# A two-block network on one core: grouped transposes, paired split products and a new order of the last expert visits, with an earlier router load and a merged final norm

## The chip, the cores and the metric

The kernel runs on one core of a Trainium2 chip. The time is that of one execution on the device, in microseconds (us), and the figure to compare is the median of several runs. The core has five engines with instruction queues of their own: TensorE (PE in the rows, with its weight loads as PEld), VectorE (DVE), ScalarE (ACT), GpSimd (POOL) and SyncE (SP), which issues almost all DMAs here. TensorE's clock has two levels, 2.4 and 1.2 GHz; the rows give the granted share (1.00 and 0.50).

## The reference, cut to what matters

A sequence of 256 tokens of width 1024 goes through two blocks of two layers each; every layer is a mixer and a feed-forward, each with a norm before it and a gated residual after it. Layer 0 has a Hyena and neighbourhood-attention mixer with a SwiGLU; layer 1 has a Fourier mixer and a mixture of experts; layers 2 and 3 have a retention and an S5 mixer, each followed by a feed-forward with a short convolution. The parts that the change touches are the mixture of experts

```python
top_val, top_idx = lax.top_k(logits, 2)              # logits: h @ w_router + b_router, 8 experts
for e in range(8):                                   # w1, w3: 1024 x 3584, w2: 3584 x 1024
    out = out + gate[..., e:e+1] * ((silu(h @ w1[e]) * (h @ w3[e])) @ w2[e])
```

and the end, `rms_norm(x) * final_norm_g`. All inputs are float32.

## The kernel before, in words

The residual stream stays in SBUF as `xT`, eight tiles of 128 channels by 256 tokens. Nearly all weights come from memory once, in tiles of about 1 MB through rings of buffers. Products at full width are split: a float32 operand becomes a rounded high part (ScalarE, `Copy` into float32r) and a remainder (VectorE, `tensor_sub`), and three float32r products replace one float32 product.

**The planner.** `Sched` records the operations of a segment, with a cost and the buffers that each reads and writes, and `flush` writes them out in the order of a list schedule: each engine takes the recorded operation that can start first, and of those that can start now the one recorded first. `matmuls` records several TensorE calls as one operation, which nothing can be put between; a `transpose` that is recorded alone is an operation of its own, with a cost of 0.065 us and 0.1 us until the next one that writes the same PSUM bank. Engines then run the emitted order in their queues, one instruction after the other.

**The experts.** With the token counts of these inputs `moe_usual` runs. It is one list of 56 visits, `VISITS`, a visit being one expert and one seventh of its hidden width: four 1 MB tiles of w1 and w3 (`up`), and two of w2, worked in `down` after the next visit's `up`. Tiles pass through 12 buffers in the order of the visits (`listed`, `used`); SyncE issues the load of tile n+12 when tile n's buffer comes free. Tokens are gathered by expert into blocks. A block of 64 tokens (T = 2) or 32 (T = 4) is the stationary operand of float32 products that use 64 or 32 columns of the array, so that two or four run side by side; `hid` records them in groups of two contraction tiles, and so does `down`. Experts 0, 3, 4, 5 have a 64-token block, experts 0, 1, 2, 6, 7 a 32-token block. Experts 1 and 2 have 128 more tokens each, whose products are split: `quarters` cuts a weight tile in four, each with a high and a low half in two of the eight `mwh` buffers, and records three products (`thirds`) for each, into the banks `h0`, `h1` in `up` and `h2`, `h3` in `down`. Between the two, the hidden values `gg` of a block are transposed in bank `t`, two or four transposes a block, and copied to `gt` (`ys` for the big blocks). After an expert's seventh visit `scatter` adds its result to `xT`, with the help of `spread`.

**Before and after the experts.** `fourier` is the segment that comes ahead of them; `route` computes the logits in it. There the router's weights `wr` go into a tile with the tag `posi`, which the tiles `odd` and the positions `posi` use before it; GpSimd clears it, then SyncE loads it. TensorE first uses it in eight products that add the shift's share of the logits to `br`; the products with `w_four` stand behind these in TensorE's order. At the other end of the kernel `finish` is a segment of its own after the last feed-forward: eight squares on ScalarE, eight products with a matrix of ones, a square root, a reciprocal, eight scalings on VectorE, and two DMAs of four tiles each.

Of the kernel before, what the change touches and what calls it, by code (L numbers as in the profile page):

```python
# [24 lines left out]
NE = 8  # L25
# [3 lines left out]
LANE = (0, 0, 0, 1, 0, 1, 1, 1)  # L29
CAPS = (3, 5, 5, 2, 2, 2, 1, 1)  # L30
VISITS = [int(c) for c in "0017031733170317317031734170"
          "4264426042644265265526552655"]


def top(e):
# [266 lines left out]
class Sched:  # L302
# [68 lines left out]
    def matmuls(self, calls):  # L371

        mm = self.tc.nc.tensor.matmul

        def run():
            for o, a, b, st, sp in calls:
                mm(_real(o), _real(a), _real(b), start=st, stop=sp, skip_group_check=True)  # L377

        if self.direct:
            run()  # L380
            return
        op = Op()
        op.eng, op.func, op.fn = "PE", None, run
        op.cost, op.lat = sum(self.cost(self.T, "matmul", c[:3], {})[0] for c in calls), 0.1
        self.add(op, [c[1] for c in calls] + [c[2] for c in calls], [c[0] for c in calls])

    def add(self, op, ins, outs):
# [172 lines left out]
class Net:  # L560
# [613 lines left out]
    def fourier(self):  # L1174
        I = self.I
        with self.segment("fourier", dict(mm=7, rt=1), pools=(1,)) as (p,):
            V, A = self.V, self.A
            cs = self.load(p, "cs", [128, 2, L])
            cl = self.load(p, "cl", [128, 2, 512])
            self.ada_until(1, 2)  # L1180
            a, b = self.scale_cols(self.mods[1], 1, self.normg[:, 2], "modA"), self.mods[1][:, 0:8]
            x, xa = self.xT, p.tile([128, 8, L], F32, name="h")
            A.activation(self.small.tile([128, 1], F32, name="warm"), x[:, 6, 0:1], AF.Sqrt, scale=0.0, bias=self.eps)
            X = p.tile([128, 4, 2, L], F32, name="fA")
            y = self.hilo(p, 8, "fy", "fy")
            sums = self.ps("rt")
            first = []
            for k in range(8):
                sq = self.small.tile([128, L], F32, name="sq", bufs=2)
                V.tensor_scalar(xa[:, k], x[:, k], a[:, k:k + 1], None, op0=OP.mult)  # L1190
                A.activation(sq, x[:, k], AF.Square)
                self.S.matmuls([(sums[:, t:t + 1], sq[:, t * 128:t * 128 + 128], self.ones[:, 0:1],
                                 k == 0 and t == 0, k == 7) for t in range(2)])
                if k % 2:
                    ps = self.ps()
                    for t in range(2):
                        self.mg(ps[:, t * L:t * L + L], [(xa[:, c, t * 128:t * 128 + 128], cs[:, c % 2])
                                                         for c in (k - 1, k)])
# [12 lines left out]
            for g in range(4):  # L1211
                ps = self.ps()
                B = [b[:, 2 * g + k:2 * g + k + 1] for k in range(2)]
                self.mg(ps[:, 0:L], [(X[:, g, tck, 0:128], cl[:, tck, 0:L]) for tck in range(2)], last=False)
                self.mg(ps[:, 0:1], [(cs[:, k, 0:128], B[k]) for k in range(2)], first=False)
                self.mg(ps[:, L:], [(X[:, g, tck, 128:256], cl[:, tck, L:]) for tck in range(2)])
                m_ = mid[32 * g:32 * g + 1]
                self.mg(m_[:, :L], [(X[:, g, tck, 128:129], cl[:, tck, 0:L]) for tck in range(2)], last=False)
                self.mg(m_[:, 0:1], [(cs[:, k, 128:129], B[k]) for k in range(2)], first=False)
                odd = p.tile([128, L], F32, name="odd", tag=("posi", "ang")[g % 2])  # L1220
                A.activation(odd, ps[:, L:], AF.Copy)
                V.memset(odd[0:1], 0.0)
                for k, op in enumerate((OP.add, OP.subtract)):
                    t = self.small.tile([128, L], F32, name="fsum")
                    V.tensor_tensor(t, ps[:, :L], odd, op)
                    if k:
                        A.activation(t[0:1], mid[32 * g:32 * g + 1, :L], AF.Copy)
                    self.put(y, 2 * g + k, t)
            self.rotary(p)
            self.s5_params(p)  # L1230
            self.ada_until(1, 3)
            route = self.route(p) if self.upto > 3 else iter(())
            next(route, None)
            self.ready = ready
            self.dense(I["w_four"], y, 8, lambda m, ps: self.residual(m, ps, 1, 2), fill=self.filler("four"))
            if self.upto > 3:
                self.moe_ahead(*self.rings)
            next(route, None)
# [99 lines left out]
    def moe_usual(self, xg, y, oh, xs, whs):  # L1338

        nc, V, A, mo, T_ = self.nc, self.V, self.A, self.mo, self.T
        S, bank, mix, ident = self.S, self.bank, self.mix, self.ident
        for e in range(1, NE):
            self.which[e] = nc.values_load(mo["ints"].real()[0:1, 1, e:e + 1], engines=(ET.SP,), min_val=0, max_val=NE - 1)
# [76 lines left out]
                                                                                       t % (T // 2) * nw + nw],  # L1422
                            i == 0, i == 7) for i in (kk, kk + 1) for t in range(T)])

        def quarters(w):

            for i in range(4):
                v = w.fold(2048)[:, 512 * i:512 * i + 512]
                h, lo = whs[turn_of("wh", 8)], whs[turn_of("wh", 8)]
                A.activation(h, v, AF.Copy)  # L1430
                V.tensor_sub(lo, v, h.bitcast(F32))
                yield i, h, lo

        def thirds(hi, lo, wh, wl):
            return [(hi, wh), (lo, wh), (hi, wl)]
# [1 line left out]
        def up(e, s):  # L1437
# [6 lines left out]
            for half in range(2):  # L1444
                for k, b, ps in st:
                    hid(k, b, ps, half, w[2 * half:2 * half + 2])
                if e in (1, 2):
                    for j in range(2):
                        for i, h, v in quarters(w[2 * half + j]):
                            kk = 4 * half + i  # L1450
                            self.mg(bank[("h0", "h1")[j]], thirds(big[0][:, kk], big[1][:, kk], h, v),
                                    first=kk == 0, last=kk == 7)
                self.used()
            for k, b, ps in st:
                gg, r, nw = self.gg[1][b // 2], rows(b), 1024 // k.T
# [8 lines left out]
        def down(e, s, st):  # L1464
            w = [self.place(self.at + i) for i in range(2)]
            for k, b, _ in st:
# [1 line left out]
                c = turn_of("gt", 2)  # L1468
                gt, ps = self.gt[:, c], bank["t"]
                m = 4 if T == 2 else 2  # L1470
                for j in range(m):
                    T_.transpose(ps[:, j * 64:j * 64 + 64], gg[r, j * 128:j * 128 + 128], ident[r, r])
                V.tensor_copy(gt[:, :64 * m], ps[:, :64 * m])
                ps = bank["a2"]
                for kk in range(0, 4, 2):
# [8 lines left out]
                    V.tensor_add(k.y, k.y, ps[:, :nd])  # L1484
            if e in (1, 2):
                ps, gg, g = bank["t"], self.gg[0][s % 2], mix["ys"][:, 0]
                for j in range(4):
                    T_.transpose(ps[:, j * 128:j * 128 + 128], gg[:, j * 128:j * 128 + 128], ident)
                A.activation(g[:, 0], ps, AF.Copy)
                V.tensor_sub(g[:, 1], ps, g[:, 0].bitcast(F32))  # L1490
                for j in range(2):
                    for i, h, v in quarters(w[j]):
                        c, d = divmod(i + 4 * j, 2)
                        q = slice(128 * c, 128 * c + 128)
                        self.mg(bank[("h2", "h3")[d]], thirds(g[:, 0, q], g[:, 1, q], h, v),
                                first=s == 0 and c == 0, last=s == 6 and c == 3)
            self.used()
            if s == 6:
                scatter(e)
# [1 line left out]
        def spread(e, k, q):  # L1501
# [8 lines left out]
            else:  # L1510
                dup = o[:, :, 0:128]
            ps = bank["t"]
            for t in range(2):
                T_.transpose(ps[:, t * 128:t * 128 + 128], dup[:, t], ident)
            self.mg(ps[:, L:L + 1], [(dup[:, t], mo["gate"][:, t, e:e + 1]) for t in range(2)])
            V.tensor_copy(mix["gs"][:, q:q + 1], ps[:, L:L + 1])
            V.tensor_copy(ots[q], ps[:, :L])
# [164 lines left out]
    def route(self, pr):  # L1682
# [2 lines left out]
        ranks = self.load(pr, "ranks", [128, NE])  # L1685
        caps = self.load(pr, "caps", [128, NE])
        prior = self.load(pr, "prior", [128, NE])
        wr = pr.tile([128, 8, 32], F32, name="w_rout", tag="posi")
        self.G.memset(wr, 0.0)
        self.Q.dma_start(wr[:, :, 0:NE], I["w_rout"])  # L1690
        br = pr.tile([128, NE], F32, name="br")
        self.Q.dma_start(br, I["b_rout"].to_broadcast([128, NE]))
        self.ada_until(1, 5)
# [270 lines left out]
    def conv_ffn(self, l, fill=None):  # L1964
        layer = 2 + l
        V, A = self.V, self.A
        with self.segment("conv", dict(mm=8), wh=1, pools=(1, 3)) as (p, pb):
# [21 lines left out]
            if l == 0:  # L1989
                fill(32)  # L1990
                self.enter(3, 0, None, [self.I["s5_in"][t] for t in range(AHEAD)])

    def rotary(self, p):
        I, V, A = self.I, self.V, self.A
# [233 lines left out]
                self.s5()  # L2228

    def finish(self):  # L2230
        with self.segment("fin", dict(mm=2)) as _:
            if self.upto >= 10:
                r = self.rstd(self.xT)
                for k in range(8):
                    self.V.scalar_tensor_tensor(self.xT[:, k], self.xT[:, k], self.normg[:, 5, k:k + 1], r,
                                                op0=OP.mult, op1=OP.mult)
            for k in range(0, 8, 4):
                self.Q.dma_start(self.out[:, k:k + 4], self.xT[:, k:k + 4])

    def run(self):  # L2240
        with self.stack:
# [16 lines left out]
            if self.upto > 5:  # L2258
                with self.phase("b"):
# [2 lines left out]
                        self.block2()  # L2262
                    if self.upto > 8:
                        self.conv_ffn(1)
            self.finish()
# [15 lines left out]
```

## Time and profile before

| | |
|---|---|
| median of 3 runs | 2314.18 us (2305.22 to 2314.53) |
| the profiled execution | 2310.9 us, span of the profile 2309.1 us, granted clock 0.97 |
| TensorE busy | 2181.6 us (94%) |
| VectorE, ScalarE, GpSimd busy | 1489.3, 983.7, 22.1 us |
| memory read | 644.7 MB, of which the experts' 336 tiles of 1 MB |
| experts' weights | first load issued at 517.3 us, the last two from 1463.7 us |

Times in the profile count from the span's start. An instruction of TensorE is shown as busy until its result is out, though the next one has long begun, so the cost of one in a stream is the distance from its start to the start of the next. A float32 product shows as two instructions, a float32r product as one. A line of a helper (L365, L377) stands for all that the planner records, so groups are told apart by the names of their tiles.

### The profile page before, as it was taken

To read this page: it belongs to the slowest core of one execution; us is meant where nothing else is said; L and a number is where in the kernel's file an instruction comes from. 1 tells how busy PE (TensorE), PEld (TensorE's weight loads), DVE (VectorE), ACT (ScalarE), POOL (GpSimd) and SP (SyncE) were. 2 spreads that over 40 slices of the span, in tenths; PEclk is the share of its full clock that TensorE was granted. 3 is DMA by queue.
4 is the path that set the end of the run, shared out by engine and by line. 5 is a ranking of instruction groups with operands and counts; after the bars stand their busy time and mean duration, and the time that the engine had idled before them with its cause. 6 is when DMAs were issued, how large, how long until landed. Compare 5 with 4: busy or idle time off the path is not lost. (4 is left out here: it accounts for less than half of the span.)

```text
span 2309.1 us, 40635 instructions
## 1 busy us (share of the span) xinstructions
PE 2181.6 (94%) x16402; PEld 1592.8 (69%) x16402; DVE 1489.3 (64%) x2806; ACT 983.7 (43%) x1724; POOL 22.1 (1%) x44
## 2 busy tenths in 40 slices
PE   7998999987999999999999999899999999879998
PEld 4787989966444454454444444379899999478997
DVE  6896889875433343454444443388959998968764
ACT  4435644453222332232323332154657656636553
POOL 0001000000000000000000000000000001000000
PEclk9999999987999999999999999899999999989999
DMA  8487489865699999988989999638646676125742
GB/s 311 169 268 174 174 341 345 304 256 208 235 387 393 420 402 420 411 327 359 419 338 418 397 420 420 260 133 314 254 167 250 218 277 236 56 109 189 253 161 94
DMA packets 103867, 651.65 MB, mean 282 GB/s; under 512 B 14087, under 2 KB 20520, under 8 KB 31160
## 3 DMA queue, kind: packets, MB, share of 16 engines
q1 hardware_dynamic: 100216, 644.26, 71.9%
q0 software_dynamic: 3456, 4.72, 1.2%
q8 instruction: 131, 2.15, 0.4%
q14 instruction: 64, 0.52, 0.1%
HBM read 644.71 MB, written 4.23 MB: 281 GB/s over the span
## 5 line engine op out<-in xcount | busy, mean ns | idle before, releaser
L377 PE MATMUL ps_mm<-hh,wh 128*128 128x256 f32 (+1 forms) x1472 | 431.6, 293 | 12.7 <-ACT hh L365 6.4
L365 ACT ACTIVATE wh<-w 128x1024 fp32r<-128x1024 f32 (+1 forms) x356 | 339.0, 979 | 239.3 <-PE ps_mm L377 183.2
L365 DVE TENSOR_TENSOR wl<-w,wh 128x1024 fp32r<-128x1024 f32 (+1 forms) x356 | 395.1, 1131 | 64.3 <-ACT wh L365 63.7
L377 PE MATMUL ps_mm<-hl,wh 128*128 128x256 f32 (+1 forms) x1472 | 422.6, 287 | 4.5 <-DVE hl L365 4.1
L377 PE MATMUL ps_mm<-hh,wl 128*128 128x256 f32 (+1 forms) x1472 | 420.1, 285 | 3.5 <-DVE wl L365 3.5
L377 PE MATMUL ps_a<-w,xg 128*32 128x256 f32 (+1 forms) x3136 | 366.4, 450 | 2.1 <-ACT xg L365 1.0
L365 DVE TENSOR_TENSOR mwh<-w,mwh 128x512 fp32r<-128x512 f32 x336 | 226.2, 690 | 123.6 <-ACT mwh L365 67.5
L365 ACT ACTIVATE mwh<-w 128x512 fp32r<-128x512 f32 x336 | 206.5, 629 | 230.1 <-PE ps_h L377 175.0
L377 PEld LDWEIGHTS ps_mm<-hh,wh 128*128 128x128 f32 x1472 | 283.0, 192 | 23.0 <-ACT hh L365 10.3
L377 PEld LDWEIGHTS ps_mm<-hl,wh 128*128 128x128 f32 x1472 | 283.4, 193 | 10.5 <-DVE hl L365 8.1
L377 PEld LDWEIGHTS ps_mm<-hh,wl 128*128 128x128 f32 x1472 | 284.2, 193 | 4.6 <-DVE wl L365 4.5
L377 PEld LDWEIGHTS ps_a<-w,xg 128*32 128x32 f32 (+1 forms) x3136 | 115.1, 117 | 157.4 <-issue 117.5
L365 DVE SCALAR_TENSOR_TENSOR w<-w,cb 128x1024 f32<-128x1024 f32 x176 | 211.7, 1220 | 6.9 <-DMA w<-in_ada_w 5.7
L377 PE MATMUL ps_h<-mwh,xs 128*128 128x512 f32 x672 | 191.8, 414 | 0.0
L377 PE MATMUL ps_a<-w,gt 128*32 128x256 f32 (+1 forms) x1568 | 183.3, 449 | 8.4 <-DVE gt L365 8.4
L377 PEld LDWEIGHTS ps_h<-mwh,xs 128*128 128x128 f32 x672 | 115.5, 188 | 61.0 <-issue 35.3
L365 ACT ACTIVATE gg<-ps_a 64x256 f32<-64x256 f32 (+1 forms) x63 | 29.8, 473 | 283.8 <-PE ps_a L377 283.8
L377 PE MATMUL ps_mm<-gh,wl 128*128 128x256 f32 x528 | 149.0, 282 | 1.6 <-DVE wl L365 1.6
L377 PE MATMUL ps_mm<-gh,wh 128*128 128x256 f32 x528 | 149.3, 283 | 0.0
L377 PE MATMUL ps_mm<-gl,wh 128*128 128x256 f32 x528 | 148.6, 281 | 0.0
L377 PEld LDWEIGHTS ps_a<-w,gt 128*32 128x32 f32 (+1 forms) x1568 | 58.3, 117 | 101.7 <-issue 63.5
L365 DVE TENSOR_TENSOR gg<-gg,ps_a 64x256 f32<-64x256 f32 (+1 forms) x63 | 33.8, 536 | 106.0 <-ACT gg L365 105.4
(452 smaller groups left out, 3369.4 us busy)
## 6 DMA issues: line engine op xcount, KB each, us to landing
w<-in_moe_w SPq DMA_DIRECT2D x336, 1024.0 KB, 11.2
w<-in_ada_w SPq DMA_DIRECT2D x88, 1024.0 KB, 6.8
w<-in_cf_up SPq DMA_DIRECT2D x44, 1024.0 KB, 5.0
w<-in_ret_in SPq DMA_DIRECT2D x24, 1024.0 KB, 4.9
w<-in_ffn_up SPq DMA_DIRECT2D x22, 1024.0 KB, 6.5
w<-in_cf_dn SPq DMA_DIRECT2D x32, 704.0 KB, 5.3
w<-in_w_in SPq DMA_DIRECT2D x12, 1024.0 KB, 8.1
w<-in_ffn_dn SPq DMA_DIRECT2D x16, 704.0 KB, 5.5
```

The costliest lines, as they stand in the source:

```text
L365: op.fn = lambda: getattr(obj, m)(*[_real(a) for a in args], **{k: _real(v) for k, v in kw.items()})
L377: mm(_real(o), _real(a), _real(b), start=st, stop=sp, skip_group_check=True)
```

## The change

It records the transposes of one block (or of one `spread`) as one operation, `turns`, with a new cost. It replaces `quarters` by `halves`: two quarters are split, and their six products are recorded as one operation; in `down` three of the six go to bank `h2` and three to `h3`. It changes the order of the last twelve visits. It gives the router's weights a tile of their own, which is cleared and loaded at the start of `fourier`. It runs `finish` inside the segment of the last feed-forward, with an early activation that uses the square root's table, and with four output DMAs of two tiles each.

```diff
-          "4264426042644265265526552655")]
+          "4264426042644265256525562556")]
...
+    def turns(self, calls):
+        tr = self.tc.nc.tensor.transpose
+        def run():
+            for o, a, i in calls:
+                tr(_real(o), _real(a), _real(i))
...
+        op.cost, op.lat = 0.18 + sum(0.165 if int(c[1].shape[0]) == 128 else 0.111 for c in calls), 0.1
+        self.add(op, [c[1] for c in calls] + [c[2] for c in calls], [c[0] for c in calls])
@@ fourier, after the loads of cs and cl @@
+            self.wr = p.tile([128, 8, 32], F32, name="w_rout")
+            self.G.memset(self.wr, 0.0)
+            self.Q.dma_start(self.wr[:, :, 0:NE], I["w_rout"])
@@ route @@
-        wr = pr.tile([128, 8, 32], F32, name="w_rout", tag="posi")
-        self.G.memset(wr, 0.0)
-        self.Q.dma_start(wr[:, :, 0:NE], I["w_rout"])
+        wr = self.wr
@@ moe_usual @@
-        def quarters(w):
+        def halves(w):
             for i in range(4):
                 v = w.fold(2048)[:, 512 * i:512 * i + 512]
                 h, lo = whs[turn_of("wh", 8)], whs[turn_of("wh", 8)]
                 A.activation(h, v, AF.Copy)
                 V.tensor_sub(lo, v, h.bitcast(F32))
-                yield i, h, lo
+                if i % 2 == 0:
+                    one = i, h, lo
+                else:
+                    yield one, (i, h, lo)
@@ moe_usual, up @@
-                        for i, h, v in quarters(w[2 * half + j]):
-                            kk = 4 * half + i
-                            self.mg(bank[("h0", "h1")[j]], thirds(big[0][:, kk], big[1][:, kk], h, v),
-                                    first=kk == 0, last=kk == 7)
+                        for two in halves(w[2 * half + j]):
+                            prods = []
+                            for i, h, v in two:
+                                kk = 4 * half + i
+                                prods += thirds(big[0][:, kk], big[1][:, kk], h, v)
+                            self.mg(bank[("h0", "h1")[j]], prods, first=kk == 1, last=kk == 7)
@@ moe_usual, down; the big blocks and spread likewise @@
-                for j in range(m):
-                    T_.transpose(ps[:, j * 64:j * 64 + 64], gg[r, j * 128:j * 128 + 128], ident[r, r])
+                S.turns([(ps[:, j * 64:j * 64 + 64], gg[r, j * 128:j * 128 + 128], ident[r, r]) for j in range(m)])
...
-                    for i, h, v in quarters(w[j]):
+                    for two in halves(w[j]):
...
+                        S.matmuls(prods)
@@ conv_ffn, at the end of its segment @@
+            else:
+                self.finish()
@@ finish @@
-        with self.segment("fin", dict(mm=2)) as _:
+        V, A, x = self.V, self.A, self.xT
+            A.activation(self.small.tile([128, 1], F32, name="warm"), x[:, 6, 0:1], AF.Sqrt, scale=0.0, bias=self.eps)
...
-            for k in range(0, 8, 4):
-                self.Q.dma_start(self.out[:, k:k + 4], self.xT[:, k:k + 4])
+                if k % 2:
+                    self.Q.dma_start(self.out[:, k - 1:k + 1], x[:, k - 1:k + 1])
```

## Rows read from the trace of the kernel before

**Rows 1.** Stretches of 20 us, all engines: busy time (instructions), granted clock, DMA share, GB/s.

```profile
1020.00:1040.00 20.00, 19.59 (x159) 8.71 (x148) 5.83 (x13) 3.08 (x6) 0.00 (x0) 1.00 0.63 241
...
1320.00:1340.00 20.00, 18.93 (x116) 8.86 (x118) 5.45 (x10) 3.72 (x6) 0.00 (x0) 1.00 1.01 420
```

**Rows 2.** Waits of 600 to 1460 us: total us, times, longest us.

```profile
ACT mwh L365 <- DMA w<-in_moe_w: 20.4, 9, 4.5
...
PE ps_a L377 <- DMA w<-in_moe_w: 1.0, 2, 0.6
```

**Rows 3.** TensorE's timeline in the experts: start us, length us, operation, [idle <-releaser].

```profile
612.43 0.27 PE L365 MATMUL ps_t<-k_ident,gg 64*128 64x64 f32 x1
...
619.05 0.86 PE L377 MATMUL ps_h<-mwh,xs 128*128 128x512 f32 x3
...
680.18 1.07 PE L377 MATMUL ps_a<-w,xg 128*32 128x256 f32 x16
681.18 0.27 PE L365 MATMUL ps_t<-k_ident,gg 64*128 64x64 f32 x1
681.38 0.96 PE L377 MATMUL ps_h<-mwh,xs 128*128 128x512 f32 x3
682.27 0.27 PE L365 MATMUL ps_t<-k_ident,gg 64*128 64x64 f32 x1
...
683.68 1.66 PE L377 MATMUL ps_h<-mwh,xs 128*128 128x512 f32 x6
685.27 1.94 PE L377 MATMUL ps_a<-w,gt 128*64 128x512 f32 x8
687.14 0.27 PE L365 MATMUL ps_t<-k_ident,gg 64*128 64x64 f32 x1
...
1434.09 0.96 PE L377 MATMUL ps_h<-mwh,xs 128*128 128x512 f32 x3
...
1447.11 0.33 PE L365 MATMUL ps_t<-k_ident,gg 64*128 64x64 f32 x2
1447.37 0.50 PE L377 MATMUL ps_a<-ot,mwh 32*128 32x256 f32 x2
```

**Rows 4.** The experts' last stretch, TensorE's timeline.

```profile
1485.31 3.65 PE L377 MATMUL ps_a<-w,gt 128*64 128x512 f32 x16 [0.82 <-DVE gt L365]
1490.57 0.38 PE L377 MATMUL ps_a<-ys,mwh 64*128 64x256 f32 x1 [1.60 <-ACT mwh L365]
```

**Rows 5.** Groups by operation, 600 to 1460 us: count | busy us, mean ns | idle before.

```profile
L365 DVE TENSOR_TENSOR mwh<-w,mwh 128x512 fp32r<-128x512 f32 x332 | 223.7, 690 | 123.6 <-ACT mwh L365 67.5 <-PE ps_h L377 53.3 <-DMA w<-in_moe_w 1.9
L365 ACT ACTIVATE mwh<-w 128x512 fp32r<-128x512 f32 x332 | 204.3, 629 | 228.8 <-PE ps_h L377 175.0 <-DMA w<-in_moe_w 20.4 <-PE ps_a L377 14.7
```

**Rows 6.** TensorE's timeline where the router's weights are first used.

```profile
513.34 2.05 PE L377 MATMUL ps_mm<-k_ident,rX 128*128 128x128 f32 x16 [1.07 <-ACT rX L365]
521.01 3.55 PE L377 MATMUL ps_mm<-w_rout,rX 128*128 128x8 f32 x16 [5.62 <-DMA w_rout<-in_w_rout]
524.42 0.56 PE L377 MATMUL ps_mm<-fyh,wh 128*128 128x256 f32 x1
```

**Rows 7.** SyncE's timeline there.

```profile
515.82 0.62 SPq L365 DMA_DIRECT2D w_rout<-in_w_rout  x1
```

**Rows 8.** Short stretches there, columns as in rows 1.

```profile
521.00:524.00 3.00, 2.99 (x15) 3.00 (x15) 2.74 (x6) 1.23 (x3) 0.00 (x0) 0.50 0.99 418
...
528.00:530.00 2.00, 2.00 (x19) 2.00 (x19) 1.49 (x5) 0.00 (x0) 0.00 (x0) 1.00 1.01 422
```

**Rows 9.** The end of the kernel, timelines of ScalarE and of TensorE.

```profile
2294.08 0.72 ACT L365 ACTIVATE sq<-xT 128x256 f32<-128x256 f32 x2 [10.08 <-PE ps_mm L377]
...
2298.70 1.28 ACT L365 ACT_TABLE_LOAD   x1
2299.99 0.47 ACT L365 ACTIVATE rstd<-ps_mm,eps 128x256 f32<-128x256 f32 x1
...
2294.71 4.72 PE L377 MATMUL ps_mm<-sq,ones 128*128 128x256 f32 x16 [0.67 <-DVE xT L365]
```

More of the change, by code (lines that the diff above doesn't have):

```diff
@@ L31 @@
 VISITS = [int(c) for c in "0017031733170317317031734170"
-          "4264426042644265265526552655"]
+          "4264426042644265256525562556"]
 def top(e):
@@ L384, in matmuls @@
         op.cost, op.lat = sum(self.cost(self.T, "matmul", c[:3], {})[0] for c in calls), 0.1
+        self.add(op, [c[1] for c in calls] + [c[2] for c in calls], [c[0] for c in calls])
[4 more added lines that the diff above has]
+                tr(_real(o), _real(a), _real(i))
+        if self.direct:
+            run()
+            return
+        op = Op()
+        op.eng, op.func, op.fn = "PE", None, run
+        op.cost, op.lat = 0.18 + sum(0.165 if int(c[1].shape[0]) == 128 else 0.111 for c in calls), 0.1
         self.add(op, [c[1] for c in calls] + [c[2] for c in calls], [c[0] for c in calls])
@@ L1338, in moe_usual @@
     def moe_usual(self, xg, y, oh, xs, whs):
-        nc, V, A, mo, T_ = self.nc, self.V, self.A, self.mo, self.T
+        nc, V, A, mo = self.nc, self.V, self.A, self.mo
         S, bank, mix, ident = self.S, self.bank, self.mix, self.ident
@@ L1486, in down @@
                 ps, gg, g = bank["t"], self.gg[0][s % 2], mix["ys"][:, 0]
-                for j in range(4):
-                    T_.transpose(ps[:, j * 128:j * 128 + 128], gg[:, j * 128:j * 128 + 128], ident)
+                S.turns([(ps[:, j * 128:j * 128 + 128], gg[:, j * 128:j * 128 + 128], ident) for j in range(4)])
                 A.activation(g[:, 0], ps, AF.Copy)
@@ L1491, in down @@
                 for j in range(2):
-                    for i, h, v in quarters(w[j]):
[L1493 to L1496, printed above, removed]
+                    for two in halves(w[j]):
+                        prods = []
+                        for d, (i, h, v) in enumerate(two):
+                            c = (i + 4 * j) // 2
+                            q = slice(128 * c, 128 * c + 128)
+                            prods += [(bank[("h2", "h3")[d]], a, b, s == 0 and c == 0 and n_ == 0,
+                                       s == 6 and c == 3 and n_ == 2)
+                                      for n_, (a, b) in enumerate(thirds(g[:, 0, q], g[:, 1, q], h, v))]
+                        S.matmuls(prods)
             self.used()
@@ L1512, in spread @@
             ps = bank["t"]
-            for t in range(2):
-                T_.transpose(ps[:, t * 128:t * 128 + 128], dup[:, t], ident)
+            S.turns([(ps[:, t * 128:t * 128 + 128], dup[:, t], ident) for t in range(2)])
             self.mg(ps[:, L:L + 1], [(dup[:, t], mo["gate"][:, t, e:e + 1]) for t in range(2)])
@@ L2230, in finish @@
     def finish(self):
-        with self.segment("fin", dict(mm=2)) as _:
[L2232 to L2236, printed above, removed]
-            for k in range(0, 8, 4):
-                self.Q.dma_start(self.out[:, k:k + 4], self.xT[:, k:k + 4])
+        V, A, x = self.V, self.A, self.xT
+        if self.upto >= 10:
+            A.activation(self.small.tile([128, 1], F32, name="warm"), x[:, 6, 0:1], AF.Sqrt, scale=0.0, bias=self.eps)
+            r = self.rstd(x)
+            for k in range(8):
+                V.scalar_tensor_tensor(x[:, k], x[:, k], self.normg[:, 5, k:k + 1], r, op0=OP.mult, op1=OP.mult)
+                if k % 2:
+                    self.Q.dma_start(self.out[:, k - 1:k + 1], x[:, k - 1:k + 1])
     def run(self):
@@ L2264, in run @@
                         self.conv_ffn(1)
-            self.finish()
 def kernel(**inputs):
```

## The prediction, written before the result

> **What bounds the kernel now.** I read the page first for the share of each engine, then the profile in stretches of 20 us, then the waits, and last TensorE's timeline, where the single runs of instructions can be told apart. The experts take some 900 of the 2309 us, and the reader is to see two things there. TensorE is busy in nearly every stretch and hardly waits: for a tile of weights its matmuls wait 1.0 us in the 860 us from 600 to 1460, and ScalarE's splitting waits 20.4 us for tiles, behind TensorE's back [rows 2]. So TensorE sets the pace. But DMA is close behind: many stretches run at 420 GB/s with a DMA share of 1.01, which is one 1 MB tile in 2.5 us or 840 us for the 336 tiles; others, as the one from 1020, fall to 241 GB/s, because SyncE waits there for a buffer that TensorE still holds [rows 1]. Of the 43 stretches of 20 us, nine are under 380 GB/s. A TensorE that gets faster can thus be followed by DMA only as far as those nine and the start leave room.
>
> Within TensorE's busy time the reader is to see what a change of kind costs. The sixteen instructions of one group of a 32-token block take 1.00 us, from 680.18 to 681.18; a group of a 64-token block takes 1.87; three split products take 0.89 from start to next start, six take 1.59; one 64-row transpose takes 0.20, two in a row 0.26 [rows 3]. The second transpose adds 0.06, so 0.14 of the 0.20 is the interruption; two threes cost 1.78 against 1.59 for a six, so 0.19 is the interruption there. Two 64-token groups in a row end after 3.65 us, one after 1.94, so the second adds 1.71 and not 1.87 [rows 3, 4].
>
> **Transposes as a group.** Between 600 and 1460 the timeline of TensorE has 183 rows of `ps_t<-k_ident,gg`, from 612.43 to 1447.11 [rows 3]. By the code there are nine small blocks and two big ones with seven visits each, 77 groups. So 106 interruptions go, at 0.14 us: 14.8 us. Where the groups on either side were of one kind they now join; I counted that at 71 of the 183 rows, which makes 41 of the 106 at 0.16, 6.6 us more. The planner will put something else there in part, so I take half of it: 18 us. Bounds: 0, if the planner's new order cuts other runs as often, and 21.4. The wait that a group adds (all operands of a block at once) is no new one, since `gt` needed the last transpose before too.
>
> **Products six at a time.** The timeline has 91 rows with three split products alone, from 619.05 to 1434.09 [rows 3]. Joined in pairs they save 45 times 0.19, 8.6 us. Against it stands the ring of eight half buffers. Before, a quarter holds two of them, so four quarters are under way; now a pair holds four, and two pairs are under way. When a pair's six products are through, ScalarE needs 0.63 and VectorE twice 0.69 before the next six in these buffers can begin [rows 5], 2.01 us, and the six themselves 1.59 less the interruption, 1.39. That is 3.40 us for a pair and 1.70 for each of two, 0.31 more than TensorE needs if it has nothing else to do. In `up` the planner has groups of other blocks to put between. In the 14 `down`s of the big experts, where up to 24 products now follow each other, the first two sixes are split ahead and the next two wait some 0.31 to 0.6: about 0.5 us each time, 7 us. I take 8.6 less 7, a gain of 2 us. Bounds: a gain of 8.6 and a loss of 168 sixes by 0.31, 52 us.
>
> **What DMA lets through** of these 20 us: in the nine slow stretches and at the start tiles can come earlier at once; in the full ones only by what TensorE's head start is short of, a few us. There is some 40 us of room in all by the slow stretches (nine of 20 us at about 300 GB/s on the mean against 420, 180 times 0.29, is 52), well above 20, but not always where it is needed. I take nine tenths, 18 us.
>
> **The order of the visits** adds and takes away no tile and no product. With expert 6 last, the tail has 256 columns where it had 512: TensorE idles 0.82 us for a `gt` and 1.60 us for the scaled result there [rows 4], and about 1 us of that should go. I take 1 us, with 3 us either way, since the last buffers come free in another order and DMA's last tiles with them.
>
> **The router's weights.** TensorE stands 5.62 us, until `w_rout` has landed; then sixteen instructions for `br` run from 521.01 to 524.42, and only behind them the products with `w_four` [rows 6]. SyncE issued that load at 515.82, right after TensorE's sixteen instructions that began at 513.34 were through [rows 6, 7]: by the code it stands behind the tile `posi`, whose place it takes. Loaded at the start of the segment, some 38 us earlier, it is no longer waited for. Two more things go with the wait: the granted clock is 0.50 from 521 to 524, after the idle time, and 1.00 from 528 [rows 8]. At full clock the sixteen instructions should take half, 1.7 us less, and the fifteen products behind them some 1.4 us less. That gives 5.6 to 8.7 us. What is late next is the splitting of the third tile of `w_four`, for which a buffer must come free; that hangs on TensorE itself and moves with it. The new load stands among a dozen small ones on SyncE, and delays those behind it by about its 0.62 us [rows 7]. I take 7 us; bounds 3 (if something on VectorE then holds the products with `w_four`) and 8.7.
>
> **The end.** The squares begin at 2294.08, the first product at 2294.71, and the square root only at 2299.99, after a table load of 1.28 us that began at 2298.70; the sixteen instructions of the products ended at 2299.43 [rows 9]. With the table loaded early the root can follow at 2299.43, 0.56 us earlier; with two squares done ahead (the buffers allow two) the products start about 0.65 us earlier. The others stay as they are, since the planner keeps work recorded earlier in front as long as TensorE has any. Gain 1.2 us. Bounds: 0.5, and 4.7 if seven squares and products go ahead, unseen.
>
> **The sum.** 18 + 1 + 7 + 1.2 is 27.2 us. The profiled execution took 2310.9 us, which gives 2283.7, say 2284. The median of the runs, 2314.18, is 3.3 us above the profiled one, and the three runs lie 9.3 us apart; so I hold 2284 against the median too.
>
> **Rivals.** (1) DMA takes it back: only in the nine slow stretches of 43 does a faster TensorE help, 20 us times 9/43, 4.2 us; then 2310.9 less 4.2, 1, 7 and 1.2 is 2297.5. For it speaks the full 420 GB/s elsewhere [rows 1], against it that TensorE's matmuls waited only 1.0 us for tiles, so they were never the slower side for long [rows 2]. (2) The change does not do what it says: the planner cuts other runs instead, and the experts gain nothing: 2301.7. For it speaks that a six that is kept whole can still stand alone between other groups, as threes do now [rows 3]. (3) Slower: the ring of eight halves. If all 168 sixes wait 0.31 us, that is 52 us against 25 to 27 gained, 2336 to 2338; it decides from about 87 of the sixes on. For it speaks that ScalarE's halves already wait 175 us for TensorE to free a buffer [rows 5]; against it that the planner knows this ring and has other groups at hand.
>
> A fourth would be the clock: that TensorE falls to 1.2 GHz after a group of transposes. The stretches with transposes in them show a granted clock of 1.00 [rows 1], but only single ones. If the group behind each of 77 ran at half clock, that would be 1.00 us each, 77 us, and 2361 us. The Trainium skill ("TensorE: Matmul & The Clock Gate", Part 4: PE-mode transpose) says that a transpose does not count as work for the clock the way a matmul does; by that rule longer groups would be a risk, and no run so far shows one in the change's place.
>
> **Chances and range.** My forecast 0.65, with a range of its own of 2266 to 2298; (1) 0.15, (2) 0.10, (3) 0.08, where between 2311 and 2338 all are possible, the clock 0.02. A measurement of this kernel can tell about 0.5% from no change, 11.6 us, so faster means under 2302.6. That holds for the forecast, for three quarters of (1) and half of (2): 0.80. Slower, above 2325.8: most of (3) and the clock, 0.07. The rest, 0.13, is the same. For 8 in 10 the range takes in all of (1) and (2) and the forecast's lower part: 2262 to 2306.
>
> **What would show it.** Right: TensorE's rows of `gg` transposes come as two or four, some 77 of them, and the 64-row group takes about 0.3 us; split products come in sixes; no wait for `w_rout`, and 1.00 clock on the first products with `w_four`; these end some 7 us earlier; the experts' last product some 25 us earlier; a table load ahead of the last products. Wrong: TensorE waits for `mwh` or for tiles in the tens of us; stretches at 420 GB/s with TensorE idle; as many rows in its timeline as before.

## The result, and the profile after

The changed kernel takes 2271.93 us (median of 4 runs, 2270.59 to 2274.97) against 2314.36 us before (4 runs): a ratio of 0.9829, 95% interval 0.9809 to 0.9848, 42.4 us less. The prediction was 2284, 30 us less than before, with a range of 2262 to 2306. The profiled execution has a span of 2268.8 us, 40.3 less than that of before.

TensorE's timeline of the changed kernel, the place that answers to [rows 3]:

```profile
682.65 3.06 PE L377 MATMUL ps_h<-mwh,xs 128*128 128x512 f32 x12
685.64 0.46 PE L393 MATMUL ps_t<-k_ident,gg 64*128 64x64 f32 x4
686.02 1.07 PE L377 MATMUL ps_a<-w,xg 128*32 128x256 f32 x16
687.03 3.02 PE L377 MATMUL ps_h<-mwh,xs 128*128 128x512 f32 x12
689.98 1.94 PE L377 MATMUL ps_a<-w,gt 128*64 128x512 f32 x8
```

Four transposes stand together and take 0.38 us from start to next start, where four single ones took 0.20 each; split products come in sixes and twelves.

Groups by operation and form in the experts, before (585 to 1500 us) and then after (578 to 1466): count | busy us, mean ns | idle before.

```profile
L377 PE MATMUL ps_h<-mwh,xs 128*128 128x512 f32 x672 | 191.8, 414 | 0.0
L377 PE MATMUL ps_a<-w,gt 128*64 128x512 f32 x448 | 108.1, 604 | 3.4 <-DVE gt L365 3.4
L377 PE MATMUL ps_h<-mwh,ys 128*128 128x512 f32 x336 | 84.5, 403 | 2.7 <-ACT ys L365 1.4 <-DVE ys L365 1.3
L377 PE MATMUL ps_a<-w,gt 128*32 128x256 f32 x1120 | 75.3, 387 | 5.0 <-DVE gt L365 5.0
L365 PE MATMUL ps_t<-k_ident,gg 64*128 64x64 f32 x182 | 42.7, 265 | 0.0
...
L365 PE MATMUL ps_t<-k_ident,gg 128*128 128x128 f32 x56 | 15.1, 313 | 0.0
```

```profile
L377 PE MATMUL ps_h<-mwh,xs 128*128 128x512 f32 x672 | 179.8, 409 | 0.1
...
L377 PE MATMUL ps_a<-w,gt 128*64 128x512 f32 x448 | 108.2, 603 | 1.5 <-DVE gt L365 1.5
L377 PE MATMUL ps_h<-mwh,ys 128*128 128x512 f32 x336 | 92.8, 412 | 0.0
L377 PE MATMUL ps_a<-w,gt 128*32 128x256 f32 x1120 | 75.1, 387 | 1.6 <-DVE gt L365 0.8 <-DVE y L365 0.8
L393 PE MATMUL ps_t<-k_ident,gg 64*128 64x64 f32 x182 | 24.7, 241 | 0.7 <-DVE gg L365 0.4 <-DVE ot L365 0.3
...
L393 PE MATMUL ps_t<-k_ident,gg 128*128 128x128 f32 x56 | 9.2, 286 | 0.0
```

The transposes cost 23.9 us less, TensorE's waits in front of the products with `gt` 5.3 less, the split products only 3.7 less (276.3 to 272.6). Of these waits those for `gt` itself fall by 6.1 us. These rows have the waits over the experts' stretch (total us, times, longest us), first before:

```profile
PE ps_a L377 <- DVE gt L365: 8.4, 14, 0.8
```

then in the changed kernel:

```profile
PE ps_a L377 <- DVE gt L365: 2.3, 5, 0.8
```

and in the experiment below that groups the transposes and nothing else:

```profile
PE ps_a L377 <- DVE gt L365: 3.6, 3, 1.7
```

Stretches of the changed kernel, for [rows 1] and [rows 8], and the waits from 600 to 1440 us, for [rows 2]:

```profile
640.00:950.00 310.00, 308.99 (x2292) 146.00 (x2284) 122.98 (x211) 94.23 (x162) 0.00 (x0) 1.00 1.01 420
...
1020.00:1040.00 20.00, 19.31 (x140) 7.67 (x138) 9.34 (x19) 4.42 (x8) 0.00 (x0) 1.00 0.64 236
...
522.00:526.00 4.00, 4.00 (x36) 4.00 (x35) 4.00 (x13) 0.42 (x1) 0.00 (x0) 1.00 1.01 422
```

```profile
ACT mwh L365 <- PE ps_h L377: 172.0, 99, 7.9
ACT mwh L365 <- DMA w<-in_moe_w: 84.5, 15, 12.3
```

DMA now runs full from 640 to 950 us (a share of 1.01 over the 310 us), and the splitting waits 84.5 us for tiles instead of 20.4; but TensorE itself still waits for none of any length.

The router's weights, TensorE and SyncE, for [rows 6, 7]:

```profile
516.63 2.05 PE L377 MATMUL ps_mm<-k_ident,rX 128*128 128x128 f32 x16 [1.07 <-ACT rX L365]
518.52 1.85 PE L377 MATMUL ps_mm<-w_rout,rX 128*128 128x8 f32 x16
520.22 0.36 PE L377 MATMUL ps_mm<-fyh,wh 128*128 128x256 f32 x1
```

```profile
481.49 0.62 SPq L365 DMA_DIRECT2D w_rout<-in_w_rout  x1
```

The wait is gone, the sixteen instructions take 1.70 us instead of 3.41, and the products behind them run at a granted clock of 1.00.

**Where the 40.3 us of the two profiled executions lie**, from the starts of the same instructions in both:

| stretch | us |
|---|---|
| up to the router's products | +3.3 |
| router's products to the last token gather at 575 | -9.3 |
| opening of the experts, to 599 | -1.3 |
| experts, 598.92 to 1490.57 before, 591.62 to 1455.96 after | -27.3 |
| last scatter and the next norm | -1.6 |
| from there to the last feed-forward | -2.7 |
| the end | -1.4 |

The first and the sixth lie in places that the change hardly touches. The sixth is clock: the falls from 1500 to 2250 us took 27.5 us before, and 24.6 in the same work after. The first is a wait and a clock fall: TensorE waited 2.46 us at 219.78 for a transfer of the attention, where it waited 0.64 before, and its granted clock is 0.50 from 221 to 224. In the traces of all the experiments below the work behind that place (from 244 us) is later than before too, by 0.5 to 2.9 us without the early load of the router's weights and by 0.6 to 4.2 with it: the profiled execution of before was the lucky one there, and whether the early load has a small share in it stays open.

### The profile page after: what moved, and what is told of

Read it like the earlier page. It is cut to its first block, busy times and chain, and to the rows that moved or that the text cites. A ratio compares the mean times of both kernels' runs of the same rounds, so it can differ in the third digit from the quotient of the medians.

```text
span 2268.8 us, 40690 instructions
## 1 busy us (share of the span) xinstructions
PE 2155.4 (95%) x16402; PEld 1586.8 (70%) x16402; DVE 1487.3 (66%) x2806; ACT 983.6 (43%) x1725; POOL 22.1 (1%) x44
## 4 chain that ended last, share of the span: by engine, by line
PE 81%; DVE 8%; DMA 6%; ACT 2%; issue 2%; SPq 0%; POOL 0%; DVEq 0%; ACTq 0%
PE ps_mm L377 39%; PE ps_a L377 22%; PE ps_h L377 11%; DMA w<-in_moe_w 3%; PE ps_hy L377 3%; PE ps_sc L377 2%; DVE a L365 2%; DVE wl L365 1%; PE ps_t L393 1%; PE ps_bu L377 1%; DVE b L365 1%; DVE w L365 1%; DMA w<-in_ada_w 1%; PE ps_o L377 1%; DMA qs<-qd 1%
## 5 line engine op out<-in xcount | busy, mean ns | idle before, releaser
L377 PE MATMUL ps_mm<-hh,wh 128*128 128x256 f32 (+1 forms) x1472 | 430.6, 293 | 12.9 <-ACT hh L365 7.2
L377 PE MATMUL ps_h<-mwh,xs 128*128 128x512 f32 x672 | 179.8, 409 | 0.1
L377 PEld LDWEIGHTS ps_h<-mwh,xs 128*128 128x128 f32 x672 | 120.2, 189 | 60.6 <-issue 31.4
```

## The experiments

The experts' stretch is measured from the 97th block-product instruction (598.92 us before; the expectations loosely call it the first) to the first product of the last scatter. It holds a few falls of the clock, at other places in each execution. In the changed kernel:

```profile
953.60:961.60 8.00, 7.80 (x38) 5.69 (x42) 7.60 (x21) 1.89 (x3) 0.00 (x0) 0.57 1.02 418
983.60:989.60 6.00, 5.20 (x64) 2.78 (x66) 2.29 (x12) 0.81 (x4) 0.00 (x0) 0.72 0.57 236
1005.60:1017.60 12.00, 12.00 (x48) 5.38 (x47) 2.27 (x5) 0.00 (x0) 0.00 (x0) 0.57 0.52 216
1171.60:1177.60 6.00, 6.00 (x56) 3.35 (x56) 2.17 (x4) 1.15 (x2) 0.00 (x0) 0.72 0.88 362
```

Length times what the granted share lacks is 3.4, 1.7, 5.2 and 1.7 us, together 12.0, so 864.35 us would be 852.4 at full clock. The table gives each kernel's stretch and what is left of it at full clock (the loss summed in stretches of 2 us); where DMA uses a slow stretch to run ahead, that is a little too low. Its last column needs no place in a trace: span times mean granted clock of the whole kernel, averaged over all its runs (4 to 19); it scatters by 1.4 to 3.0 us from run to run, so that a mean of 4 runs is good to some 2.5 us and one of 10 or more to some 1.5. The full-clock figure of the stretch comes from one execution each: before, visits alone and both ends alone, whose experts differ in the tail at most, lie 1.7 us apart, so a difference of 2 us in that column tells nothing by itself. Each ratio is to the runs of before that were made beside the kernel (medians 2312.02 to 2315.28), and the first line has the median of the result above.

| kernel | median us | ratio to before, interval | changes of kind | stretch | at full clock | whole kernel, span x clock |
|---|---|---|---|---|---|---|
| before | 2314.36 | | 749 | 891.65 | 886.3 | 2242.4 |
| changed | 2271.93 | 0.9829 (0.9809 to 0.9848) | 585 | 864.35 | 852.4 | 2199.6 |
| turns alone | 2282.57 | 0.9864 (0.9823 to 0.9904) | 558 | 861.95 | 850.0 | 2204.3 |
| sixes alone | 2319.64 | 1.0028 (1.0009 to 1.0046) | 748 | 902.69 | 888.9 | 2243.4 |
| visits alone | 2313.24 | 1.0005 (0.9990 to 1.0021) | 749 | 895.62 | 888.0 | 2239.9 |
| both ends alone | 2301.87 | 0.9952 (0.9934 to 0.9970) | 749 | 895.11 | 887.9 | 2236.0 |
| changed, threes | 2270.62 | 0.9817 (0.9775 to 0.9858) | 556 | 861.88 | 846.2 | 2195.3 |
| threes, four tiles | 2257.47 | 0.9754 (0.9720 to 0.9787) | 436 | 847.51 | 837.3 | 2186.7 |
| sixes, four tiles | 2264.13 | 0.9791 (0.9764 to 0.9817) | 447 | 856.24 | 838.4 | 2187.4 |
| before, half tiles | 2308.38, one run | | 749 | 891.15 | 884.3 | |
| changed, half tiles | 2271.42, one run | | 585 | 862.65 | 846.3 | |
| four tiles, half tiles | 2232.59, one run | | 436 | 827.37 | 822.3 | |

A change of kind is a place in the order of TensorE's instructions where one of another sort follows: a block product of 32 or of 64 columns, a product at full width, a transpose, a product of a scatter. How finely the sorts are told apart moves the counts a little. By the part of the array that an instruction uses, with transposes apart, the same stretch has 777 before, 599 in the changed kernel, 578 with turns alone, 770 with sixes alone, 578 with threes and 446 with four tiles; so a price per change below is good to about a tenth.

**Turns alone**: the kernel before, with the transposes grouped.

```diff
-                for j in range(m):
-                    T_.transpose(ps[:, j * 64:j * 64 + 64], gg[r, j * 128:j * 128 + 128], ident[r, r])
+                S.turns([(ps[:, j * 64:j * 64 + 64], gg[r, j * 128:j * 128 + 128], ident[r, r]) for j in range(m)])
```

> The kernel before with the grouped transposes alone (blocks, big blocks and the spreads, with the new cost); products stay in threes. In the instruction order of TensorE the experts have 749 changes of kind before, 585 in the changed kernel and 558 here. Theory A (each change of kind costs TensorE 0.14 to 0.19 us and nothing else matters much): 191 changes fewer are 27 to 36 us, so the stretch from the first block product to the first product of the last scatter, 891.65 us before and 864.34 in the changed kernel, takes 856 to 865 here, and the time is 2279 to 2288. Theory B (the forecast's sizes, the rest of the gain being the sixes and the new order of visits): 14.8 to 18 us, so 874 to 877 us, and 2296 to 2300.

861.95 us and 2282.57 us: theory A. The grouped transposes alone bring 29.7 us in the experts, or 36.3 at full clock, 0.19 for each of 191 changes. That is more than the whole change brings there. Not all of it is the interruption itself: the waits for `gt` are 4.8 us less here, as shown above.

**Sixes alone**: the kernel before, with `halves` for `quarters`.

```diff
-                        for i, h, v in quarters(w[2 * half + j]):
+                        for two in halves(w[2 * half + j]):
```

> The kernel before with the six products as one operation alone; transposes stay single. The instruction order has 748 changes of kind against 749 before. Theory A (changes of kind): the experts' stretch stays at 889 to 894 us, and the time within 3 us of before. Theory B (the sixes save their interruptions, as forecast): 8.6 us less to 2 us less, 883 to 890. Theory C (the ring of eight halves): TensorE waits for the halves, 7 us or more, 899 us and up.

902.69 us: outside A and B as it ran, and in C's region. But TensorE does not wait in front of these products, as the groups of this kernel show (585 to 1510 us):

```profile
L377 PE MATMUL ps_h<-mwh,xs 128*128 128x512 f32 x672 | 181.5, 409 | 0.0
L377 PE MATMUL ps_h<-mwh,ys 128*128 128x512 f32 x336 | 93.7, 413 | 2.5 <-ACT ys L365 1.5 <-DVE ys L365 0.9
```

The products take 275.2 us where they took 276.3. At full clock the stretch is 2.5 us longer than before, and the whole kernel, over its ten runs, 1.0, both within the scatter: 8.5 of the stretch's 11.0 us are the clock. So at full clock the sixes are worth nothing, as A has it, and the ring is not what costs. As it ran, the kernel is 6.9 us slower than its runs of before (2312.76), and its interval leaves out 1; A's 3 us did not hold. Nearly all of that loss is the clock's, which is taken up below.

**Both ends alone**: the early load of the router's weights and `finish` in the last feed-forward.

```diff
+            self.wr = p.tile([128, 8, 32], F32, name="w_rout")
...
+            else:
+                self.finish()
```

> The kernel before with the router's weights loaded early and the last norm and output in the last feed-forward, nothing else. The experts' instruction order is that of before. If the two parts are independent of the others: the products with the router's weights and the first ones behind them end 8.9 us earlier against the work ahead of them, the end is 1.4 us shorter, and the time is about 10 us less, 2304. If the 3 us that the changed kernel lost between 215 and 246 us come from this part, they are there again and the time is about 2307; if they are an accident of that execution, they are not.

10.9 us less than the 2312.76 of its own runs of before, as expected; at full clock it is 6.4, so some of this was the clock's; it stood at 0.50 behind the wait for the weights [rows 8]. From the end of the work ahead to the seventh product with `w_four`'s remainder it is 4.3 us, as in the changed kernel (4.0); before it is 12.9. The 3 us between 215 and 246 us are there again in this execution (3.6 from 244 us), but without the early load they are in part there too, as said above, and the time is 2302 and not 2307.

**The changed kernel with threes.**

```diff
-                        for two in halves(w[2 * half + j]):
+                        for i, h, v in quarters(w[2 * half + j]):
```

> The changed kernel with the products in threes again (four quarters of a tile), all else as changed. The instruction order has 556 changes of kind against 585 in the changed kernel. Theory A (changes of kind): 29 fewer at 0.14 to 0.19 are 4 to 5.5 us, so the experts' stretch takes 859 to 861 us against 864.34, and the time is 2266 to 2268. Theory B (the sixes gain, as forecast): 2 to 8.6 us more than the changed kernel, 866 to 873 us, 2274 to 2280.

861.88 us, 2.5 less than with sixes, and 846.2 at full clock, 6.2 less; the whole kernel at full clock is 4.3 us shorter. That is A's sign, and its size, 4 to 5.5 us, lies between the 2.5 as it ran and the 6.2; the forecast's gain from sixes is not there. But the medians, 2270.62 and 2271.93, cannot be told apart.

**Four contraction tiles as one operation**, with threes.

```diff
-            for kk in range(4 * half, 4 * half + 4, 2):
-                S.matmuls([(ps[M * t:M * t + M, :nw], k.x(i), ...
-                            i == 0, i == 7) for i in (kk, kk + 1) for t in range(T)])
+            S.matmuls([(ps[M * t:M * t + M, :nw], k.x(i), ...
+                        i == 0, i == 7) for i in range(4 * half, 4 * half + 4) for t in range(T)])
```

> The changed kernel with products in threes, and with the block products of four contraction tiles, not two, recorded as one operation in both halves of an expert. The instruction order has 436 changes of kind in the experts, against 556 with threes alone and 585 in the changed kernel. Theory A (TensorE's changes of kind set the time): 120 fewer at 0.2 us are 24 us, so the experts' stretch, 861.88 us with threes alone, takes 835 to 841, and the time is about 2247. Theory D (DMA takes it back): 324 tiles at 2.5 us are 810 us at the full 420 GB/s, and the changed kernel is short of that rate by some 53 us in all, of which the start and the tail hold more than half; so at most 10 us of the 24 are seen, 852 to 860 us, and the time is 2258 to 2268.

847.51 us and 2257.47 us, between the theories: 14.4 of A's 24 us came as it ran, and 8.9 at full clock, which is within D's 10. It is faster than both kernels. Now TensorE waits for tiles, 7.9 us in seven waits (waits of this kernel, 600 to 1440 us, then its timeline and a stretch):

```profile
ACT mwh L365 <- DMA w<-in_moe_w: 100.3, 19, 13.4
PE ps_a L377 <- DMA w<-in_moe_w: 7.9, 7, 2.4
```

```profile
1305.05 0.34 PE L393 MATMUL ps_t<-k_ident,gg 64*128 64x64 f32 x2
1307.77 1.93 PE L377 MATMUL ps_a<-w,xg 128*32 128x256 f32 x32 [2.38 <-DMA w<-in_moe_w]
```

```profile
1300.00:1320.00 20.00, 17.20 (x150) 9.16 (x146) 9.26 (x16) 7.56 (x13) 0.00 (x0) 1.00 1.01 421
```

**Half tiles**: in three kernels only half of each tile is loaded from the thirteenth on, the order of all instructions kept.

```diff
         self.Q.dma_start(v, src)
+        if not self.S.direct and n >= 12 and e is not None:
+            obj, c = self.Q.obj, shape[0] // 2
+            self.S.ops[-1].fn = lambda: obj.dma_start(_real(v[:, 0:c]), src[:, 0:c])
```

> The kernel before, with only half of each expert tile loaded from the thirteenth on (the other half keeps what was there; the result is not the reference's), in the same order of instructions on every engine. Theory A (TensorE alone sets the experts' pace before): the stretch stays at 884 to 889 us at full clock, 888 to 900 with what the clock takes. Theory D (tiles hold TensorE up in gaps that the trace does not show): more than 10 us less, 876 or below at full clock.

> The changed kernel, with only half of each expert tile loaded from the thirteenth on, same order of instructions. Theory A: the experts' stretch stays at 849 to 854 us at full clock, where the changed kernel has 852.4. Theory D (DMA has become the bound in the fourteen of twenty stretches that run at 420 GB/s): it gets shorter by 8 us or more, 844 or below.

> The kernel with four contraction tiles as one operation, with only half of each expert tile loaded from the thirteenth on. Both theories have TensorE alone here: 120 changes of kind fewer than with threes alone, 846.2 us at full clock, at 0.2 us each, so 820 to 826. What this run is below the one with whole tiles is what DMA holds back: nothing by theory A, 15 us or more by theory D.

At full clock 884.3, 846.3 and 822.3 us, that is 2.0, 6.0 and 15.0 us below the same kernels with whole tiles (by the whole kernel at full clock, one run each, 2.7, 4.9 and 18.4). Before, TensorE alone set the pace (A). In the changed kernel DMA holds some 6 us, between the theories; with four tiles it holds 15 (D). TensorE's idle time in the stretch says where: it falls by 0.7, 1.7 and 12.7 us (16.2 to 15.5, 9.6 to 7.9, 20.6 to 7.9), so that with four tiles most of the 15 us are seen as waits, and in the changed kernel most of the 6 are not; how much of them is scatter stays open. The same stretch of the last kernel with half tiles:

```profile
1300.00:1320.00 20.00, 20.00 (x112) 8.93 (x110) 8.74 (x14) 6.62 (x11) 0.00 (x0) 1.00 0.63 211
```

With DMA out of the way TensorE gains 38.0 us for 164 changes and 24.1 for the next 149: 0.23 and 0.16 us each, with what the waits gained in it.

**Visits alone.**

```diff
-          "4264426042644265265526552655")]
+          "4264426042644265256525562556")]
```

> The kernel before with the new order of the last twelve visits alone. The instruction order has 749 changes of kind in the experts, as before. Theory A: only the tail changes, where the last scatters have 24 groups of one sort instead of 30; the experts' stretch takes 3 to 4 us less than the 886.3 us that the kernel before has at full clock, and the time is 2309 to 2312. Theory B (the forecast's): 1 us less. Theory C (buffers come free in another order and the last tiles are late): 1 to 3 us more.

1.0005, and 888.0 us at full clock where before has 886.3; over the whole kernel 1.9 less than in its own runs of before (2241.8). Nothing that can be told from no change: A's 3 to 4 us do not show, and B's 1 us is too small to see. The tails suggest why. From 1479 us on before has waits of 0.52, 0.82 and 1.60 us, 2.9 together, ahead of the last scatter ([rows 4] has the last two); with the visits alone there are six from 1483 on, 2.4 us together, and in the changed kernel seven from 1443 on, 2.9 us together (three of them below).

```profile
1444.74 1.94 PE L377 MATMUL ps_a<-w,gt 128*64 128x512 f32 x8 [0.57 <-DVE gt L365]
...
1449.60 1.93 PE L377 MATMUL ps_a<-w,gt 128*32 128x256 f32 x32 [0.79 <-DVE y L365]
...
1455.96 5.19 PE L377 MATMUL ps_a<-ys,mwh 32*128 32x256 f32 x16 [0.28 <-DVE xT L365]
```

**Sixes with four tiles**: both groupings in one kernel, the changed one with the edit for four tiles alone.

> The changed kernel, sixes kept, with the block products of four contraction tiles as one operation. The instruction order has 447 changes of kind in the experts against 436 with threes. Theory A (a six costs by the changes of kind that the planner makes around it): 11 changes are 2 us, so 838 to 841 us at full clock where threes have 837.3, and the time is 2256 to 2261. Theory C (the ring of eight halves stalls the sixes once TensorE has fewer groups to put between): 843 us or more, 2263 and up.

838.4 us at full clock, 1.2 more than with threes, and 0.7 over the whole kernel: A. The time, 2264.13, is C's, but not for C's reason: the mean clock of its four runs is 0.9665 against 0.9695, and all but 0.7 of the 6.7 us are that.

## Why the prediction was right, and what it got wrong

The time lay in the range and the main mechanism was right: TensorE set the pace of the experts, and what it gained is the interruptions that went and some waits. The term that was mis-sized is the experts' 18 us: 33.9 at full clock, 27.3 as it ran. It is most of the 12 us by which the forecast fell short.

- **Transposes as a group.** The price held. The group's 23.9 us of busy time hold 0.07 us of overlap for each of 105 rows that went (a single one is shown for 0.27 us and the next starts after 0.20), which leaves 16.5; the forecast had 14.8. It failed in two places. It took half of the groups that join on either side, 3.3 us; of the 164 changes of kind that went, some 105 are these rows, and the other 59 are some 9 us at 0.16. And "the wait that a group adds is no new one" priced the wait at nothing, while waits went: TensorE's for `gt` fall from 8.4 to 2.3 us, and to 3.6 with the turns alone, so that most of this is the grouping. That single transposes, spread among other work, had delayed `gt` is the likely reason; no run shows it apart.
- **Products six at a time.** A gain of 2 us was forecast; none is seen, alone or with the turns. The fault is the count: the 91 lone threes (the trace has 97) were to be joined, but the kernel with sixes alone has 748 changes of kind against 749, and 154 unbroken runs of split products against 159. The planner puts nearly as many other groups between sixes as between threes: 140 of the 154 runs are a lone six. The ring's waits, the cost in the forecast, do not show either.
- **What DMA lets through.** Nine tenths were forecast; 33.9 of 38.0 is 0.89. The factor came out right, the amount that it was laid on was half of what TensorE gained. In part that is luck, since the forecast had argued the nine tenths for 20 us and not for 38.
- **The order of the visits.** 1 us forecast, 3 either way: alone it gives nothing that can be measured. The waits of the tail were hardly taken away, but spread.
- **The router's weights.** 7 us forecast, upper bound 8.7; the wait of 5.62, 1.7 for the sixteen instructions and 1.4 for the products behind came in full, 8.9 from the comparison above. The caution about VectorE was not needed.
- **The end.** 1.2 us forecast, 1.4 measured, by another route. Not two but seven squares and products go ahead (changed kernel, one such product among TensorE's, then ScalarE's end):

```profile
2253.15 0.27 PE L377 MATMUL ps_mm<-gh,wl 128*128 128x256 f32 x1
2253.26 0.59 PE L377 MATMUL ps_mm<-sq,ones 128*128 128x256 f32 x2
2253.51 0.47 PE L377 MATMUL ps_mm<-gh,wh 128*128 128x256 f32 x1
2253.81 0.28 PE L377 MATMUL ps_mm<-gl,wh 128*128 128x256 f32 x1
```

```profile
2245.07 1.28 ACT L365 ACT_TABLE_LOAD   x1
...
2258.17 0.42 ACT L365 ACTIVATE sq<-xT 128x256 f32<-128x256 f32 x1 [1.59 <-DVE xT L365]
2259.37 0.47 ACT L365 ACTIVATE rstd<-ps_mm,eps 128x256 f32<-128x256 f32 x1 [0.79 <-PE ps_mm L377]
```

From 2253.26 to `gl` at 2253.81 it is 0.55 us, where a step of this stream is 0.12; six such insertions put off the feed-forward's last products by 2.5 us. The root starts 1.8 us after these have ended, where it took 6.0 [rows 9]. The one eats most of the other: the bound of 4.7 for seven products ahead left out what they cost TensorE, which is the engine that ends last there.

**The rivals.** (1) DMA took back little (4.1 of the 38.0 us), but it is next: it holds some 6 us in the changed kernel and 15 with four tiles. (2) The planner did not undo the gain: 749 changes of kind became 585. But with grouped transposes it cuts more runs for sixes than for threes, 585 against 556, which fits the 4 to 6 us that threes are shorter at full clock. (3) The ring did not stall TensorE. The clock did not fall behind the groups as such: in the changed kernel, from 640 to 950 us, with grouped transposes all through, it stays at 1.00. The Trainium skill ("TensorE: Matmul & The Clock Gate", Part 4: PE-mode transpose) says that transposes do not count as work for the clock the way matmuls do; in this stretch groups of two and four between products do no harm, and no run shows longer ones. Two other kernels leave a question: with four tiles the clock falls near 660 us, right behind a wait of 2.41 us that follows a pair of transposes (its timeline and a stretch),

```profile
659.35 5.35 PE L377 MATMUL ps_a<-w,xg 128*64 128x512 f32 x16 [2.41 <-DVE gg L365]
```

```profile
660.40:664.40 4.00, 4.00 (x14) 0.98 (x9) 0.83 (x3) 0.00 (x0) 0.00 (x0) 0.57 0.98 406
```

and with threes near 755, behind a wait of 2.39 us a little after a pair; yet behind the wait of 2.38 us at 1307.77, shown above, which follows a pair too, it stays at 1.00. What part a pair and the wait have in such a fall stays open.

For the cost of a change of kind the Trainium skill has a rule without a number ("TensorEngine Tiling (Array Packing)", Key Properties: changing the tiling mode drains the engine). The runs are in line with it: a change costs 0.16 to 0.23 us here, waits included. That the cost is a drain, they do not show.

## What to carry to other kernels

Count the changes of kind in the order in which the instructions are issued, before and after an edit, and price them by two rows of one stream (one alone, two in a row); here that count foretold the sign of every grouping at full clock, and it showed before the run that the sixes join next to nothing. Group what is smallest and stands alone most often first: the 0.06 us transposes, then the block products, which gave 9 us more at full clock. When the engine that sets the pace gets faster, load half the bytes once, in the same order of instructions: it tells in one run how far the other bound is, to within the scatter of one execution (some 2 us here).

## What was not expected of the hardware

The clock moves these kernels by as much as some of the parts do. It took back 6.6 of the 33.9 us in the two profiled executions. In the changed kernel two of its four falls in the experts begin among the products of scatters (near 954 and 1005), and two in block products that stand right behind gathers or a scatter (near 985 and 1173); the other kernels have falls elsewhere too, as the one near 660 above. The fall near 1005 in the changed kernel's timeline, the clock 0.50 from about 1005.6:

```profile
1003.63 0.50 PE L377 MATMUL ps_a<-ot,mwh 32*128 32x256 f32 x2 [0.25 <-DVE xT L365]
...
1004.92 0.50 PE L377 MATMUL ps_a<-ys,mwh 128*128 128x256 f32 x2
1005.35 0.57 PE L377 MATMUL ps_a<-ot,mwh 32*128 32x256 f32 x2
1005.85 0.79 PE L377 MATMUL ps_a<-ys,mwh 128*128 128x256 f32 x2
```

Not every change of kind costs the same. Before, three split products take 0.70 us from start to next start behind a product of a gather, which uses the full width too (median of 9), and 0.89 behind a block product or a 64-row transpose (medians of 42 and 28).

Whether sixes bring more falls, which is what their 6.9 us alone would be, stays open: the mean clock is 0.968 with sixes alone (10 runs) against 0.970 (19 of before), and 0.9665 against 0.9695 with four tiles, but in the changed kernel 0.9688 with sixes against 0.9675 with threes (4 runs each).
